# Where the gate products of a softmax attention stage are placed among its steps

## The chip, the cores and the metric

One core of a Trainium2 chip runs the whole program. The metric is the device time of one execution in microseconds (us), the median of several executions. Engines are named as the profile names them: PE (matmuls), PEld (PE's weight loads, which run beside the matmuls), DVE (VectorE), ACT (ScalarE), POOL (GpSimd), SP (which here issues most of the loads).

## The reference, cut to what matters

A trunk of two layers over 1040 frames of 1024 features. Each layer has an attention part and a gated feed-forward part. The attention part has two groups of heads that read the same normalised input: a gated linear attention ("GLA", 4 heads of 128 values) and a softmax attention with a forgetting bias ("FoX", 8 heads of 64). The GLA result is multiplied by a gate that comes from a product of its own:

```python
gq, gk, gv, gr, glr, fq, fk, fv, ff = jnp.split(xn @ w_in[i], cuts, axis=-1)
...
o_gla = rms_norm(o_gla, gla_norm[i].reshape(GLA_HEADS, GLA_DV)).reshape(B, L, GLA_WIDTH)
o_gla = o_gla * jax.nn.silu(gr)
...
h = h + jnp.concatenate([o_gla, o_fox], axis=-1) @ w_out[i]
```

The four 128-wide blocks of `gr` are the four gates of this document. Nothing of the softmax needs them: they are wanted only by the output projection `w_out`.

## The kernel before, in words

Activations lie transposed: features on 128 partitions, frames along the free dimension. Every dense product is made three times with split operands (high weight by high input, low by high, high by low: `mm3`, L254 to L256). One 128-wide weight tile by a chunk of frames takes 8 blocks of features, so 24 matmuls; the attention's products use the three chunks `CH_FOX` of 344, 348 and 348 frames.

Weights come by `weights` (called for each tile): two loads of 256 KB by SP (L212), for each half a cast to the high part on ACT (L221), and a subtraction for the low part (L223). The subtraction runs on POOL inside the attention stage (`self.att` set, `self.mixing` not) and on DVE elsewhere. There are three buffers each for high and low halves, so one tile and a half.

The attention stage of a layer runs GLA first. While the second pair of GLA heads is stepped through, the products of the first FoX head pair are made beside it, and at its end the weights of one more tile are already brought in (`coming`, next to the last `gla_steps`).

Then `fox` runs the softmax: four head pairs, each of 18 steps, from long rows of scores to short ones (row tiles 8 and 7, then 6 and 5, and so on, for two heads). One step is: scores on PE (L690, L691), bias and running minimum on DVE (L693), exponential on ACT (L705), two steps later transposes on PE (L726) that ACT and DVE copy and split (L368, L369), and three steps later the product with the values (L752). A loop over slots, `n` from 0, gives each slot one step and what earlier steps left due.

Beside the steps, dense products are dealt out as filler. A `Work` object is a queue of generators, one for each tile and chunk (`add_tile`, `unit`), with `left`, the summed cost in the kernel's own figures (`mm_us`, 3.54 us for a chunk of 348 frames). In every slot `fox` computes `fill_us`, the remaining cost over the remaining slots, and runs that much. `plan(p)` makes the queues: queue p begins at slot `starts[p]`, that is 4 slots after head pair p has begun (slots 4, 22, 40, 58), and the last at slot 62; what is left of the queue before is drained there. `plan(-1)` holds for slots 0 to 3 and is empty. Queues 0 to 2 hold the q, k and v products of the next head pair (9 chunks), then one gate (3 chunks). Queue 3 holds the last gate, and queue 4 the first part of the output projection. In `unit` the first use of a tile also starts the weights of the tile behind it in the same queue.

A gate chunk (`gr_products`) ends in an evacuation: DVE L650, L653, L657, L658, L659, L661, ACT L654 to L656, a load of the GLA result (L647, SP) and a store of the gated result (L663, POOL).

In this stage the order of instructions on an engine isn't the order of the source alone: the planner of the framework may issue an instruction ahead of its place when it takes its engine to be free, and prefers what stands earlier in the source. (The feed-forward stage writes PE's order by hand; the attention doesn't.) [...]

## Time and profile before

| what | us |
|---|---|
| median of 3 runs | 2505.76 (2503.37 to 2509.76) |
| the profiled execution, whole | 2508.55 |
| its span, first to last instruction | 2506.7 |
| PE busy in the span | 2470.6 |
| DVE busy | 1836.5 |
| ACT busy | 1296.8 |
| POOL busy | 385.6 |

The times of rows below count from the start of the span. The first layer's softmax begins its scores at 176.19 us. A busy PE is not PE at its peak: the profile models the ends of matmuls, and matmuls overlap one another. In the tables by stretch each engine has its busy time and, in brackets, its instructions that began in that stretch; then come the granted PE clock, the share of the DMA engines and what they moved.

### The profile page before, as it was taken

The page shows a single profiled execution, that of the slowest core. Times are in us where ns is not written, and L with a number is a line of the kernel's source. Part 1 is how long each engine was busy: PE and PEld are TensorE (multiplying, and loading weights), DVE is VectorE, ACT ScalarE, POOL GpSimd, SP SyncE. Part 2 cuts the span into 40 slices and gives each one's busy share as a digit, 9 for nine tenths or more (in the row PEclk, how much of TensorE's full clock was granted, in tenths as well). Part 3 has the DMA queues.
Part 4 walks back from the last instruction along what each step waited for, and adds up shares of the span by engine and source line. Part 5 has one row for each costly group of instructions (what it writes and reads, how often), then busy time and mean ns, then how long its engine had stood idle before and what let it go on. Part 6 is the DMA issues. An engine that isn't in the chain of part 4 may idle for free.

```text
span 2506.7 us, 47344 instructions
## 1 busy us (share of the span) xinstructions
PE 2470.6 (99%) x18358; PEld 2375.5 (95%) x18358; DVE 1836.5 (73%) x3739; ACT 1296.8 (52%) x2811; POOL 385.6 (15%) x567
## 2 busy tenths in 40 slices
PE   9999999999999999999999999999999999999998
PEld 8999999999999999999999899999999999997786
DVE  8656776869988888853566666777799888887535
ACT  7346666646555555641343566665465555555412
POOL 2023333210000000100211233431100000001002
PEclk9999999999999999999999999999999999999999
DMA  3132134343322224763312222143432222348622
GB/s 130 64 94 68 46 97 129 123 125 103 115 81 73 89 69 155 189 179 102 107 58 68 75 78 74 65 147 109 149 98 85 89 81 85 102 149 184 191 62 74
DMA packets 118546, 260.97 MB, mean 104 GB/s; under 512 B 14881, under 2 KB 32545, under 8 KB 118321
## 3 DMA queue, kind: packets, MB, share of 16 engines
q1 hardware_dynamic: 93984, 182.79, 23.5%
q0 software_dynamic: 22464, 72.84, 10.4%
q8 instruction: 144, 2.36, 0.4%
q10 hardware_dynamic: 1872, 2.31, 0.3%
q14 instruction: 82, 0.66, 0.1%
HBM read 177.29 MB, written 67.81 MB: 98 GB/s over the span
## 4 chain that ended last, share of the span: by engine, by line
PE 68%; issue 17%; DVE 9%; ACT 4%; DMA 2%; POOL 1%; SPq 0%; DVEq 0%; POOLq 0%; ACTq 0%
PE mm L254 7%; PE mm L256 7%; PE mm L255 7%; PE up L254 5%; PE up L255 5%; PE up L256 5%; PE down L254 5%; PE down L255 5%; PE down L256 5%; PE av L752 3%; PE tr L726 2%; DVE S L693 1%; PE wo L254 1%; PE wo L256 1%; PE wo L255 1%
## 5 line engine op out<-in xcount | busy, mean ns | idle before, releaser
L254 PE MATMUL up<-x,hi 128*128 128x260 f32 (+1 forms) x2240 | 634.0, 283 | 0.0
L256 PE MATMUL up<-x,hi 128*128 128x260 f32 (+1 forms) x2240 | 632.5, 282 | 0.7 <-DVE x L1157 0.7
L255 PE MATMUL up<-x,lo 128*128 128x260 f32 (+1 forms) x2240 | 632.5, 282 | 0.0
L256 PEld LDWEIGHTS up<-x,hi 128*128 128x128 f32 x2240 | 422.9, 189 | 1.1 <-DVE x L1157 0.9
L254 PEld LDWEIGHTS up<-x,hi 128*128 128x128 f32 x2240 | 422.2, 188 | 0.5 <-DVE hg L1370 0.2
L255 PEld LDWEIGHTS up<-x,lo 128*128 128x128 f32 x2240 | 422.5, 189 | 0.1
L254 PE MATMUL mm<-xh,hi 128*128 128x348 f32 (+4 forms) x1056 | 363.1, 344 | 0.0
L256 PE MATMUL mm<-xl,hi 128*128 128x348 f32 (+4 forms) x1056 | 340.0, 322 | 0.0
L255 PE MATMUL mm<-xh,lo 128*128 128x348 f32 (+4 forms) x1056 | 339.4, 321 | 0.0
L1133 DVE TENSOR_TENSOR lo<-raw,hi 128x512 fp32r<-128x512 f32 (+1 forms) x434 | 266.4, 628 | 81.0 <-ACT hi L1132 80.1
L1132 ACT CAST hi<-raw 128x512 fp32r<-128x512 f32 (+1 forms) x434 | 243.2, 572 | 148.1 <-PE up L256 88.7
L254 PEld LDWEIGHTS mm<-xh,hi 128*128 128x128 f32 x1056 | 199.6, 189 | 5.5 <-issue 4.6
L255 PEld LDWEIGHTS mm<-xh,lo 128*128 128x128 f32 x1056 | 199.5, 189 | 0.7 <-issue 0.7
L256 PEld LDWEIGHTS mm<-xl,hi 128*128 128x128 f32 x1056 | 198.4, 188 | 0.4 <-issue 0.3
L221 ACT CAST hi<-raw 128x512 fp32r<-128x512 f32 (+2 forms) x168 | 97.3, 580 | 187.4 <-PE down L256 106.0
L255 PE MATMUL down<-ah,lo 128*128 128x260 f32 (+1 forms) x528 | 168.8, 320 | 0.0
L254 PE MATMUL down<-ah,hi 128*128 128x260 f32 (+1 forms) x528 | 168.6, 319 | 0.0
L256 PE MATMUL down<-al,hi 128*128 128x260 f32 (+1 forms) x528 | 168.5, 319 | 0.0
L705 ACT ACTIVATE P<-S,m 116x460 f32<-116x460 f32 (+2 forms) x224 | 124.7, 561 | 71.7 <-DVE m L693 68.1
L369 DVE TENSOR_TENSOR PT<-tr,PT 116x464 fp32r<-116x464 f32 (+3 forms) x240 | 123.1, 516 | 47.3 <-ACT PT L368 45.7
L1114 DVE TENSOR_TENSOR raw<-raw,raw 128x512 f32<-128x512 f32 x198 | 135.3, 689 | 28.6 <-DMA raw<-in_wd_dram 26.4
L1395 POOL DMA_DIRECT2D actd<-cv x44 | 23.5, 535 | 744.4 <-DVE cv L1394 726.3
(308 smaller groups left out, 5974.7 us busy)
## 6 DMA issues: line engine op xcount, KB each, us to landing
raw<-in_wm_dram SPq DMA_DIRECT2D x330, 256.0 KB, 3.0
raw<-in_wd_dram SPq DMA_DIRECT2D x64, 256.0 KB, 3.5
actd<-cv POOLq DMA_DIRECT2D x22, 520.0 KB, 3.0
actd<-cv POOLq DMA_DIRECT2D x22, 512.0 KB, 3.0
cb<-cd SPq DMA_DIRECT2D x16, 520.0 KB, 3.8
st<-actd SPq DMA_DIRECT2D x14, 520.0 KB, 4.7
st<-actd SPq DMA_DIRECT2D x14, 512.0 KB, 5.0
kA<-kA SPq DMA_DIRECT2D x24, 260.0 KB, 4.1
```

Source lines behind the costliest of these rows:

```text
L221: nc.scalar.copy(hi[:, :n, :], raw[:, :n, :])
L254: nc.tensor.matmul(ps, wh, xh[:, c0:c0 + n], start=first, stop=False, skip_group_check=more)
L255: nc.tensor.matmul(ps, wl, xh[:, c0:c0 + n], start=False, stop=False, skip_group_check=more)
L256: nc.tensor.matmul(ps, wh, xl[:, c0:c0 + n], start=False, stop=last, skip_group_check=more)
L369: nc.vector.tensor_tensor(out=lo, in0=src, in1=hi.bitcast(F32), op=ALU.subtract)
L693: nc.vector.tensor_tensor_reduce(out=S[:rows, :n], in0=S[:rows, :n], in1=cb[:rows, c0:k1], scale=1.0, scalar=(BIG if ci == 0 else m[:rows, ...
L705: nc.scalar.activation(P[:rows, :n], S[:rows, :n], AF.Exp, scale=-1.0, bias=m[:rows, nch - 1:nch], accum_out=(den if nch == 1 else d3[:row ...
L726: nc.tensor.transpose(tr[:w, 3 - j, :rows], P[:rows, o:o + w], id_)
L752: nc.tensor.matmul(av[:, a:b], w.rearrange("p a b -> p (a b)"), x, start=(t == ts[0] and part == 0 and i == 0), stop=(t == last and i == 1))
L1114: nc.vector.tensor_tensor(out=q[out][:, :nk, :], in0=q[a][:, :nk, :], in1=q[b][:, :nk, :], op=op)
L1132: nc.scalar.copy(hi[:, :nk, :], src[:, :nk, :])
L1133: nc.vector.tensor_tensor(out=lo[:, :nk, :], in0=src[:, :nk, :], in1=hi[:, :nk, :].bitcast(F32), op=ALU.subtract)
```

## The change

The products of gate 0 move from the end of queue 0 to the queue of slots 0 to 3, which was empty; the weights that are brought in ahead during the GLA part are now those of gate 0 and no longer those of the q product of the second head pair. The six chunks of gates 1 and 2 are dealt out two to a queue: queue 0 ends with chunks 0 and 1 of gate 1, queue 1 with chunk 2 of gate 1 and chunk 0 of gate 2, queue 2 with chunks 1 and 2 of gate 2. A gate that is spread over two queues has its weights brought in twice. `tail` is the cost of the gate chunks at the end of a queue: while more than that is left, the rate is set so that the q, k and v products are done half a slot before the next head pair begins; the two gate chunks then go over the four slots that follow.

```diff
     def __init__(self):
-        self.q, self.left, self.boxes, self.debt = [], 0.0, [], 0.0
+        self.q, self.left, self.boxes, self.debt, self.tail = [], 0.0, [], 0.0, None
...
-    def gr_products(self, lyr, h, work, ap, pp, nm, dst=None):
+    def gr_products(self, lyr, h, work, ap, pp, nm, dst=None, w=None, chunks=CH_FOX):
...
-        self.add_tile(work, pp, self.wm[lyr, M_GR + h], nm["x"], CH_FOX if dst is None else CH_FOX[::-1], ev)
+        self.add_tile(work, pp, self.wm[lyr, M_GR + h], nm["x"], chunks, ev, w=w)
...
             fill_us = work.left / max(starts[p_next] - n, 1)
+            if work.tail is not None and work.left > work.tail:
+                fill_us = (work.left - work.tail) / max(first[p_next] - 0.5 - n, 0.5)
...
-                coming = {"src": self.wm[lyr, M_FQ + 1], "slots": None}
+                coming = {"src": self.wm[lyr, M_GR], "slots": None}
...
                     if p < 0:
-                        return w
-                    if p < 3:
-                        self.fox_products(lyr, p + 1, w, ap, pp, nm, qs[p + 1], None if p else coming["w"])
-                        self.gr_products(lyr, p, w, ap, pp, nm)
+                        self.gr_products(lyr, 0, w, ap, pp, nm, w=coming["w"])
+                    elif p < 3:
+                        self.fox_products(lyr, p + 1, w, ap, pp, nm, qs[p + 1])
+                        w.tail = -w.left
+                        for h, some in (((1, CH_FOX[:2]),), ((1, CH_FOX[2:]), (2, CH_FOX[:1])), ((2, CH_FOX[1:]),))[p]:
+                            self.gr_products(lyr, h, w, ap, pp, nm, chunks=some)
+                        w.tail += w.left
...
-                        self.gr_products(lyr, 3, w, ap, pp, nm, land[3])
+                        self.gr_products(lyr, 3, w, ap, pp, nm, land[3], chunks=CH_FOX[::-1])
```

## The prediction

> **What bounds the kernel now.** I read the page first, then the busy time by stretches through the softmax of each layer, then the waits of the worst stretch.
>
> ```profile
> PE 2470.6 (99%) x18358; PEld 2375.5 (95%) x18358; DVE 1836.5 (73%) x3739; ACT 1296.8 (52%) x2811; POOL 385.6 (15%) x567
> PE 68%; issue 17%; DVE 9%; ACT 4%; DMA 2%; POOL 1%; SPq 0%; DVEq 0%; POOLq 0%; ACTq 0%
> ```
>
> PE is busy for 99% of the span and carries 68% of the chain that ended last. The change takes no matmul away, so it can only win where PE loses time now. To find those places I compare stretches with a quiet one.
>
> ```profile
> 176.00:186.00 10.00, 9.76 (x62) 8.82 (x61) 5.73 (x22) 5.50 (x17) 3.73 (x5) 1.00 0.38 114
> 186.00:198.00 12.00, 10.77 (x74) 9.08 (x73) 8.78 (x30) 9.08 (x26) 4.50 (x7) 1.00 0.01 1
> 198.00:210.00 12.00, 11.66 (x89) 11.07 (x88) 8.76 (x27) 8.54 (x27) 2.60 (x4) 1.00 0.00 1
> ...
> 250.00:260.00 10.00, 10.00 (x66) 9.25 (x65) 7.99 (x28) 6.91 (x25) 2.72 (x5) 1.00 0.18 57
> 260.00:270.00 10.00, 9.88 (x68) 8.94 (x67) 9.66 (x30) 8.22 (x25) 3.41 (x6) 1.00 0.18 54
> 270.00:280.00 10.00, 10.00 (x75) 9.87 (x74) 8.50 (x28) 6.93 (x22) 3.21 (x5) 1.00 0.36 120
> ...
> 340.00:350.00 10.00, 9.89 (x67) 8.72 (x67) 9.72 (x31) 8.52 (x28) 2.83 (x4) 1.00 0.12 37
> 350.00:360.00 10.00, 10.00 (x76) 9.87 (x75) 9.66 (x32) 6.37 (x19) 3.82 (x6) 1.00 0.36 119
> ...
> 370.00:410.00 40.00, 39.89 (x288) 39.30 (x288) 22.55 (x75) 22.52 (x70) 16.32 (x23) 1.00 0.35 95
> ...
> 420.00:430.00 10.00, 9.86 (x66) 8.66 (x65) 9.71 (x35) 9.07 (x29) 2.33 (x5) 1.00 0.20 58
> ...
> 450.00:460.00 10.00, 8.25 (x61) 7.98 (x59) 10.00 (x33) 9.78 (x28) 3.16 (x6) 0.95 0.25 73
> ```
>
> After the bounds and the length stand PE, PEld, DVE, ACT and POOL. In the quiet stretch 370 to 410 weight loads run for 39.30 of 40 us, 98.3%, because nearly every matmul has one beside it; so a shortfall of PEld against 98.3% measures lost time even where PE still counts as busy. Three places stand out. **The early stretch**, the first eight steps of the first head pair: PE idles 0.24 + 1.23 + 0.34 = 1.81 us, and PEld falls short by 1.01 + 2.72 + 0.73 = 4.46 us. **The turns**, where a new head pair begins while the gate before it is still being made: there DVE is nearly full (9.66, 9.72 and 9.71 of 10). At the first turn PE idles 0.12 us and PEld is short by 0.58 + 0.89 = 1.47 us; the other two turns show 1.11 and 1.17 us in their worst ten us. **The end** (450 to 460), where PE idles 1.75 us; the work there is queue 4, which the change leaves alone.
>
> The second layer's early stretch, and what PE waits for in the first layer's:
>
> ```profile
> 1419.00:1429.00 10.00, 9.97 (x65) 9.02 (x63) 6.83 (x23) 6.08 (x18) 3.11 (x6) 1.00 0.24 79
> 1429.00:1441.00 12.00, 10.46 (x72) 8.94 (x71) 8.90 (x29) 9.14 (x29) 3.29 (x6) 1.00 0.00 1
> 1441.00:1453.00 12.00, 12.00 (x94) 11.78 (x93) 8.38 (x31) 8.69 (x28) 3.30 (x5) 1.00 0.07 23
> ```
>
> ```profile
> PEld S L690 <- ACT P L705: 2.3, 5, 0.9
> ...
> PE S L690 <- ACT P L705: 1.1, 2, 0.7
> ```
>
> Here the idle is 0.03 + 1.54 = 1.57 us and the shortfall 0.81 + 2.86 + 0.02 = 3.69 us. Between 186 and 198 PE waits for the exponentials of earlier scores: the softmax runs alone, with no dense matmul to put between. Why is there none?
>
> ```profile
> 176.19 0.45 PE L690 MATMUL S<-kA,qA 128*116 128x460 f32 x1
> ...
> 178.26 0.40 PE L254 MATMUL mm<-xh,hi 128*128 128x344 f32 x1
> ...
> 183.07 0.32 PE L255 MATMUL mm<-xh,lo 128*128 128x348 f32 x1
> 183.23 0.32 PE L256 MATMUL mm<-xl,hi 128*128 128x348 f32 x1
> ...
> 190.54 0.32 PE L254 MATMUL mm<-xh,hi 128*128 128x348 f32 x1
> ```
>
> This is PE in order of time. Step 0's scores start at 176.19. At 178.26, long before slot 4, q products of the second head pair begin: the planner already pulls filler into slots 0 to 3. That is two of nine chunks, gone by about 190, and then slots 4 to 6 find their share used up. The rows also give the price of filler: matmuls start 0.16 us apart, so a chunk is 24 x 0.16 = 3.8 us.
>
> **The change part by part.**
>
> *Gate 0 into slots 0 to 3.* It adds 3 x 3.8 = 11.5 us of PE work to the early stretch, against 1.8 idle or 4.5 short: ample. What its evacuation adds on the other engines:
>
> ```profile
> L650 DVE TENSOR_TENSOR gx<-mm,r x24: 506/510/518, 253.5 to 1695.1; 128x348 f32<-128x348 f32 x16, 128x344 f32<-128x344 f32 x8
> L653 DVE TENSOR_SCALAR ge<-gx x24: 328/338/1021, 254.5 to 1695.9; 128x348 f32<-128x348 f32 x16, 128x344 f32<-128x344 f32 x8
> L657 DVE TENSOR_TENSOR gog<-gx,gog x24: 505/510/516, 254.9 to 1696.2; 128x348 f32<-128x348 f32 x16, 128x344 f32<-128x344 f32 x8
> L658 DVE SCALAR_TENSOR_TENSOR ge<-ge,gy x24: 506/516/521, 257.1 to 1699.5; 128x348 f32<-128x348 f32 x16, 128x344 f32<-128x344 f32 x8
> L659 DVE SCALAR_TENSOR_TENSOR gy<-ge,gy x24: 510/521/1464, 257.7 to 1700.6; 128x348 f32<-128x348 f32 x16, 128x344 f32<-128x344 f32 x8
> L661 DVE SCALAR_TENSOR_TENSOR gog<-gy,gog x18: 500/514/603, 258.3 to 1678.0; 128x348 f32<-128x348 f32 x12, 128x344 f32<-128x344 f32 x6
> ```
>
> By the medians a gate chunk is 0.51 + 0.34 + 0.51 + 0.52 + 0.52 + 0.51 = 2.91 us of DVE, three are 8.7. The early 34 us hold 23.3 us of DVE now; 32.0 us in 34 + 11.5 - 3 = 42.5 us is 75%. ACT has 23.1 us there and room for three short operations a chunk. So the filler is covered, and what ends is the wait between 186 and 198. Bounds of the gain: the idle alone, 1.7 a layer (mean of 1.81 and 1.57), and the whole shortfall, 4.1 (4.46 and 3.69). I take the shortfall of the one stretch where the waits stand, 2.72 and 2.86: **2.8 us a layer**. The gate's load and store (SP, POOL) are the same instructions, earlier; nothing in slots 0 to 3 reads them.
>
> *One chunk fewer at each turn.* PE gives up 3.8 us, DVE 2.91. The first turn has DVE 7.99 + 9.66 + 8.50 = 26.15 of 30; afterwards it is 23.2 in 26.2, so 89% and not 87%: the turn gets shorter, not looser. Where DVE sets the pace, it shortens by 2.91 only and PE loses 3.8 - 2.9 = 0.9 more. Bounds a layer: a gain of all the shortfall (about 1.47 + 1.11 + 1.17 = 3.8) and a loss of 3 x 0.9 = 2.7. I take a gain of the idle only, 0.12 + 0.11 + 0.14 = **0.4 us a layer**: with DVE's share unchanged, the rest has no reason to go.
>
> *More weight loads.* Before, 11 tiles a layer pass through POOL; after, 13: gates 1 and 2 come twice. The q weights of the second pair no longer lie ready at slot 4.
>
> ```profile
> L221 ACT CAST hi<-raw x28: 607/620/661, 161.5 to 453.4; 128x512 fp32r<-128x512 f32 x28
> L223 POOL TENSOR_TENSOR lo<-raw,hi x22: 1272/1292/1419, 176.8 to 409.0; 128x512 fp32r<-128x512 f32 x22
> DMA to landing us min/median/max: 2.5/2.7/6.3
> ```
>
> A half costs 0.62 us on ACT and 1.29 on POOL, so the four new ones cost 2.5 and 5.2 us a layer. POOL is under 45% in every stretch quoted and hides its part; ACT has room in the quiet stretch (22.52 of 40), where two of the four casts fall, and less at a turn (9.07 of 10), where exponentials would queue behind the other two: 1.2 us at most, kept in the range. What they can cost PE besides comes by way of DVE:
>
> ```profile
> 267.08 1.46 DVE L659 SCALAR_TENSOR_TENSOR gy<-ge,gy 128x348 f32<-128x348 f32 x1
> ...
> 270.45 1.02 DVE L653 TENSOR_SCALAR ge<-gx 128x348 f32<-128x348 f32 x1
> ```
>
> ```profile
> 266.87 1.30 POOL L223 TENSOR_TENSOR lo<-raw,hi 128x512 fp32r<-128x512 f32 x1
> ...
> 269.96 1.30 POOL L223 TENSOR_TENSOR lo<-raw,hi 128x512 fp32r<-128x512 f32 x1
> ```
>
> Each of the two gate operations on DVE overlaps a subtraction on POOL and is longer than its median, by 0.94 and 0.68 us. [...] From the rows alone: bounds 0 and 4 x 0.94 = 3.8 us of DVE. Two of the four halves (gate 2's in queue 1) fall among gate operations, 2 x 0.81 = 1.6 us, and DVE is full in about a third of a turn: **0.5 us a layer lost**.
>
> *Sum.* 2.8 + 0.4 - 0.5 = 2.7 us a layer, 5.4 for both: the profiled execution goes from 2508.55 (span 2506.7 and 1.9 around it) to 2503.2. It ran 2.8 us above the median; from the median, 2505.76 - 5.4 = **2500.4 us**.
>
> **The rivals.**
>
> *Weights late (slower).* At slot 4 the q weights, and in slots 36 to 39 two tiles of a single chunk each, must be cast and subtracted while PE nears them; the second half waits for a buffer that the tile before still holds. With both halves exposed, 2 x (0.62 + 1.29) = 3.8 us at three places, 11.5 a layer less the 2.7: 17.6 us more, 2523. It wins from 0.9 us at each place on. Against it: at slot 22 the same happens today, and with the last gate chunk's matmul at 267.93 the next tile's begins here, scores and transposes filling the time between:
>
> ```profile
> 267.93 0.32 PE L256 MATMUL mm<-xl,hi 128*128 128x348 f32 x1
> ...
> 270.11 0.40 PE L254 MATMUL mm<-xh,hi 128*128 128x344 f32 x1
> ```
>
> *Turns starved (no change).* DVE sets the turns, the loss of 2.7 comes true: -2.8 + 2.7 + 0.5 = 0.4 a layer, 2506.6. For it: DVE at 97%. Against: PE still counts 9.86 or more of 10 there.
>
> *The planner undoes it (no change).* It already pulls filler forward, so gate 0 may only push out what was pulled, with the hole a few slots later: 2505.8. Against: slots 0 to 6 now own 11.5 us more.
>
> *All shortfall returns (faster).* 4.1 + 3.8 - 0.5 = 7.4 a layer: 2491.0. [...] The trace so far shows waits for only a part of it.
>
> **How the numbers follow.** Forecast (2 to 9 us gained) 0.46, weights late 0.17, the two of no change 0.24, all returned 0.13. About 0.3%, 7.5 us, is what a measurement of this kernel can tell from no change. Half of the forecast's chance lies beyond it: faster 0.23 + 0.13 = 0.36; same 0.23 + 0.22 = 0.45; slower 0.17 + 0.02 = 0.19. The range reaches from 2489 (all returned, with 2 us of spread between runs) to 2512 (no change, or one late tile a layer), and leaves out most of the slower rival, 0.18 in all. The interval of the forecast alone is 2497 to 2504.
>
> **What would show it.** Right: between the tenth and the twenty-second us of the first head pair PE has next to no wait for ACT, PEld is at 11.5 or more of 12, gate matmuls run from slot 0, and 26 subtractions on POOL a layer. Turns: the same DVE share in a shorter turn. Wrong: q matmuls of the second pair that wait for a subtraction (L223), a hole after slot 4 or at the turns, or L659 and L653 stretched more often. If PE's idle time in the early stretch goes and the time stays, the turns or the end took it.

## The result and the profile after

The changed kernel takes **2518.76 us** in the median of five runs (2516.5 to 2522.58); the kernel before takes 2509.76 in five runs (2503.37 to 2510.51). The ratio of the means is 1.0045, 95% interval 1.0034 to 1.0057: slower by under half a percent, where 2500.4 was predicted, a gain of 5.4 us. The profiled execution took 2518.76 us, its span 2517.0, which is 10.3 us more than before.

The page of the kernel after:

```profile
span 2517.0 us, 47386 instructions
...
PE 2470.7 (98%) x18358; PEld 2372.0 (94%) x18358; DVE 1842.4 (73%) x3739; ACT 1302.9 (52%) x2819; POOL 397.4 (16%) x575
```

PE runs the same 18358 matmuls and counts as busy for the same time, 2470.7 against 2470.6 us. So the 10.3 us are time in which PE idles that it did not idle before. I look for it where the change was made: first in the early stretch. The rows give, after the bounds and the length, PE, PEld, DVE, ACT, POOL, then granted clock, DMA share and GB/s (as in the prediction). The first head pair begins 1.75 us earlier than before, so the bounds are shifted by about 2.

```profile
174.00:184.00 10.00, 9.77 (x63) 8.88 (x62) 6.39 (x25) 5.01 (x16) 2.81 (x4) 1.00 0.34 114
184.00:196.00 12.00, 11.99 (x79) 10.84 (x78) 11.36 (x34) 9.94 (x28) 4.07 (x6) 1.00 0.18 53
196.00:208.00 12.00, 12.00 (x90) 11.70 (x88) 10.01 (x27) 8.06 (x21) 4.98 (x8) 1.00 0.24 82
```

PE is busy for 11.99 of the 12 us in which it idled 1.23 before; weight loads rose from 9.08 to 10.84, less than the 11.5 that the prediction set as a sign. This part of the change does what it says, though not in full. Then the places where a new head pair begins. From here on a **turn** is the stretch from the first scores of a head pair to those of its seventh step, six steps long; the other twelve steps are the **rest** of the pair. **Filler** is the dense matmuls of the queues alone. The bounds are read from PE's rows in time; for the first turn (second head pair) they are, before and after:

```profile
249.69 0.42 PE L690 MATMUL S<-kA,qA 128*116 128x460 f32 x1
...
279.32 0.38 PE L690 MATMUL S<-kA,qA 128*116 128x460 f32 x1
```

```profile
256.83 0.42 PE L690 MATMUL S<-kA,qA 128*116 128x460 f32 x1
...
284.61 0.38 PE L690 MATMUL S<-kA,qA 128*116 128x460 f32 x1
```

With such bounds, busy time by stretches for the first layer of the kernel before: opening of pair 0, its rest, turn 1, rest, turn 2, rest, turn 3.

```profile
176.19:200.02 23.83, 22.02 (x144) 19.01 (x142) 16.14 (x53) 15.95 (x47) 8.23 (x12) 1.00 0.16 49
200.02:249.69 49.67, 49.39 (x362) 48.62 (x361) 29.48 (x98) 30.41 (x91) 18.60 (x25) 1.00 0.29 80
249.69:279.32 29.63, 29.50 (x202) 27.68 (x202) 26.15 (x84) 21.53 (x70) 8.81 (x14) 1.00 0.24 78
279.32:331.38 52.06, 51.98 (x376) 51.19 (x375) 30.03 (x95) 30.99 (x91) 22.27 (x29) 1.00 0.27 79
331.38:360.96 29.58, 29.47 (x202) 27.65 (x202) 26.14 (x84) 21.53 (x70) 8.84 (x14) 1.00 0.23 78
...
413.03:443.35 30.32, 30.18 (x205) 28.20 (x205) 27.14 (x90) 23.88 (x75) 9.31 (x18) 1.00 0.40 134
```

And the same stretches of the kernel after:

```profile
174.44:204.81 30.37, 30.12 (x201) 27.87 (x199) 25.10 (x73) 21.36 (x60) 9.96 (x15) 1.00 0.27 89
204.81:256.83 52.02, 51.96 (x376) 51.16 (x375) 29.94 (x95) 30.63 (x90) 21.65 (x28) 1.00 0.28 82
256.83:284.61 27.78, 26.49 (x180) 23.80 (x178) 23.38 (x78) 20.78 (x68) 8.35 (x14) 1.00 0.22 66
284.61:336.68 52.07, 52.00 (x377) 51.21 (x375) 29.93 (x95) 30.75 (x90) 22.11 (x29) 1.00 0.28 81
336.68:365.57 28.89, 26.36 (x179) 23.85 (x179) 25.12 (x78) 21.59 (x70) 11.51 (x16) 1.00 0.26 83
...
417.65:447.95 30.30, 27.06 (x181) 24.27 (x181) 24.54 (x83) 22.23 (x72) 8.57 (x17) 1.00 0.43 142
```

These two tables are the whole result. Pair 0 grows from 73.50 to 82.39 us, by **8.89** for three chunks (24 matmuls at 0.16 us each, 3.84 us a chunk, 11.5 for three), so 2.6 us are won there. Each turn loses one chunk (turns 1 and 2 fall from 96 filler matmuls to 72, turn 3 from 99 to 75), and is shorter by **1.85, 0.69 and 0.02 us** where 3.84 were given up. The rests of the later pairs do not move. In the first layer this makes 8.89 - 2.56 = 6.3 us more; in the second the turns save 1.9, 0.7 and 1.61, which makes 4.7 more. From the first scores to the first output projection matmul of queue 4 the stage takes 285.9 and 284.2 us in the two layers against 279.3 and 279.5: 11.3 us of the span's 10.3. All else differs by one microsecond in sum, the other way (1947.0 us against 1948.0).

How to read the loss: PEld falls in turn 1 by 27.68 - 23.80 = 3.88 us, about the chunk that left, but the stretch shortens by 1.85 only. Against the quiet stretch's 98.3% the shortfall rises from 1.45 to 3.51 us. PE's idle time rises from 0.13 to 1.29 in turn 1, 0.11 to 2.53 in turn 2, 0.14 to 3.24 in turn 3. What left was work that had covered waits of the softmax; without it the waits show. In turn 1 ACT's exponentials wait for DVE's running minimum for 3.7 us in the kernel before and for 3.8 in the kernel after: that wait was there already, beside a busy PE.

DVE, which the prediction took to set the turns' pace, did lose its work as reckoned (26.15 to 23.38 in turn 1, where 23.2 was forecast), but its share of the turn fell to 84%, where 89% was forecast: the turn did not shorten as much as DVE's work.

What PE waits for in turn 1 of the kernel after (total, times, longest), which names only part of the 1.29 us:

```profile
PE tr L791 <- DVE PT L369: 0.5, 1, 0.5
PE S L690 <- ACT P L705: 0.5, 1, 0.5
```

No wait of a gate or q matmul for a cast or a subtraction stands there, in turns 2 and 3 or in the early stretch. Turn 3 of the first layer has a cause of its own: the bias rows of the last pair land late and PE stands for 2.21 us (last section); in the second layer, without that wait, turn 3 gave back 1.61.

### The profile page after: what moved, and what is told of

It reads as the page before. It is cut to its first block, busy times and chain, and to the rows that moved or that the text cites. A ratio compares the mean times of both kernels' runs of the same rounds, so it can differ in the third digit from the quotient of the medians.

```text
span 2517.0 us, 47386 instructions
## 1 busy us (share of the span) xinstructions
PE 2470.7 (98%) x18358; PEld 2372.0 (94%) x18358; DVE 1842.4 (73%) x3739; ACT 1302.9 (52%) x2819; POOL 397.4 (16%) x575
## 3 DMA queue, kind: packets, MB, share of 16 engines
q0 software_dynamic: 22464, 72.84, 10.3%
```

## The experiments

The theory after the result is **local worth**: a matmul given to a stretch where PE is full costs its 0.16 us, but a matmul taken out of a turn gives back less, because there the softmax's own way (scores, minimum, exponential, transposes, copies) and the gate's evacuation need the time anyway. What the edits do is read from the stage's length, because all else in the program takes 1942.5 to 1955.6 us in these kernels (those with other banks aside), a spread as large as the loss. Rivals, tried one after another: the second fetching of weight tiles; the way the filler is spread; the evacuation load on DVE and ACT; the number of score banks; too short a lag between the softmax's steps; the planner, which moves work between stretches.

This table has the lengths that the text below uses, in us, worked out as above from each run's rows. "Left" is the number of filler matmuls in turn 1. The stage is that of the first and second layer.

| run | pair 0 | turn 1 (left) | turn 2 | turn 3 | stage |
|---|---|---|---|---|---|
| before | 73.5 | 29.6 (96) | 29.6 | 30.3 | 279.3 / 279.5 |
| after | 82.4 | 27.8 (72) | 28.9 | 30.3 | 285.9 / 284.2 |
| e4_early_more | 82.4 | 29.6 (96) | 29.6 | 30.1 | 287.9 / 288.3 |
| e3_turn_less | 71.1 | 29.0 (87) | 29.0 | 31.1 | 271.6 / 272.3 |
| e1_even_pace | 79.7 | 29.0 (87) | 30.2 | 31.9 | 282.3 / 283.6 |
| e5_queue_from_0 | 75.6 | 29.2 (84) | 29.6 | 30.2 | 280.9 / 281.5 |
| e9_one_chunk_early | 73.8 | 29.6 (90) | 29.6 | 30.3 | 279.7 / 279.5 |
| e6_slim_after | 82.4 | 27.3 (72) | 26.3 | 30.0 | 282.4 / 280.2 |
| e7_slim_before | 73.5 | 29.5 (96) | 29.5 | 30.0 | 278.8 / 278.8 |
| e8_two_tiles_later | 82.4 | 27.8 (72) | 27.8 | 27.8 | 282.7 / 282.5 |

**The two halves of the change, one at a time.** The first kernel does the three chunks early and takes nothing away later: gate 0 is made twice, once in slots 0 to 3 and once where it was.

```diff
                     if p < 0:
+                        self.gr_products(lyr, 0, w, ap, pp, nm, w=coming["w"])
                         return w
                     if p < 3:
-                        self.fox_products(lyr, p + 1, w, ap, pp, nm, qs[p + 1], None if p else coming["w"])
+                        self.fox_products(lyr, p + 1, w, ap, pp, nm, qs[p + 1])
```

> The kernel before with gate 0 made once more in slots 0 to 3 (its products computed twice, queues 0 to 2 as before, the weights brought in ahead those of gate 0). The price of the early part alone: by the prediction 11.5 us of PE work less 2.8 to 3 us of filled waits, so 8 to 9 us a layer, less the 1.75 us by which the first scores begin earlier in the changed kernel: 14 to 17 us for both layers. If the q weights that are no longer ready at slot 4 cost something, more than 11.5 us a layer, 23 us and up. Head pair 0 becomes about 82 us, as in the changed kernel; pairs 1 and 2 stay at 81.7.

Measured 2522.34 us against 2507.7, ratio 1.0067 (1.0054 to 1.008): 14.6 us for six chunks of 3.84, and the stage is longer by 8.6 and 8.8 (all else was 3.9 us shorter in the profiled execution). The turns stay as they were. So the early term holds by itself: three chunks cost 8.7 us a layer in place of 11.5, and some 2.8 are won.

The second does the other half alone: before, with one chunk fewer in each of the first three gates, nothing moved and no tile brought in twice.

```diff
+                if c0 == CH_FOX[1][0]:
+                    nc.gpsimd.dma_start(self.mixd[h][:, c0 + n:T], og)
-        self.add_tile(work, pp, self.wm[lyr, M_GR + h], nm["x"], CH_FOX if dst is None else CH_FOX[::-1], ev)
+        self.add_tile(work, pp, self.wm[lyr, M_GR + h], nm["x"], CH_FOX[:2] if dst is None else CH_FOX[::-1], ev)
```

> The kernel before with the third chunk of gates 0 to 2 left out (its place in the stored mix is filled with the second chunk's values): every turn has one chunk less, nothing else is moved and no tile is brought in twice. If a chunk at a turn is worth its PE time, as the prediction had it, the time falls by 6 x 3.9 = 23 us, head pairs 1 and 2 from 81.7 to about 77.8 us. Theory 'starved turn': a chunk is worth 0.5 to 2 us there, pairs 1 and 2 stay above 79.5 us, and the time falls by 3 to 12 us only. Theory 'weights': since no tile is added here, the full 23 us.

Measured 2495.56 us, ratio 0.9955 (0.9943 to 0.9968): 12 us for six chunks worth 23 us of PE. The starved turn had 3 to 12 us, so this is its upper end, and pairs 1 and 2 fell to 78.3 us where it had them above 79.5. Nothing is fetched twice here, so the double fetching cannot be the main cause. Busy time of turn 1, the rest behind it, and turn 3:

```profile
246.80:275.76 28.96, 28.50 (x196) 26.48 (x196) 23.96 (x81) 21.49 (x70) 10.61 (x16) 1.00 0.26 77
275.76:325.14 49.38, 49.24 (x358) 48.48 (x357) 28.55 (x92) 30.02 (x88) 20.17 (x28) 1.00 0.30 84
...
403.51:434.56 31.05, 29.16 (x202) 27.53 (x202) 25.50 (x87) 22.84 (x74) 9.53 (x17) 1.00 0.42 142
```

The even pacing takes the 24 filler matmuls from both parts of the pair, 15 from the rest and 9 from the turn; three transposes that follow the v product move from the rest into the turn. So the rest does 18 matmuls fewer: its weight loads fall by 51.19 - 48.48 = 2.71 us and it shortens from 52.06 to 49.38, by 2.68: full worth. The turn does six fewer: its weight loads fall by 27.68 - 26.48 = 1.20 us and it shortens by 0.67, about half. That is local worth, seen on both sides in one run. The chunk's evacuation has left too, so this run doesn't tell the two reasons apart. Turn 3 even grows by 0.7; DVE waits 3.8 us for the bias rows there (see the last section).

**The same work, spread evenly.** After, without the tail's own pace:

```diff
-                        w.tail = -w.left
...
-                        w.tail += w.left
```

> The changed kernel without the pacing of the queues: the eleven chunks of queues 0 to 2 go evenly over 18 slots (2.16 us of filler a slot, and no longer 2.36 until half a slot before the next pair and 1.77 after). Theory 'starved turn' (a turn has too little dense work beside a softmax that is paced by DVE and ACT, so a chunk taken from it saves much less than its 3.8 us of PE): head pairs 1 and 2 stay within 1.5 us of the changed kernel's 79.8 and 81.0 us and the time stays some 8 to 12 us above the kernel before. Theory 'pacing' (the slower rate in the four slots of the turn makes the hole): pairs 1 and 2 fall to about 77.9 us each (before less one chunk), and the time is 2 to 6 us under the kernel before. Theory 'weights' (tiles brought in twice, POOL stretching DVE): no change against the changed kernel, pair 2 stays about 1 us above pair 1.

Measured 2512.93 us, ratio 1.0024 (1.0015 to 1.0033), half of the loss; of the three expectations none had it (8 to 12 us slower, 2 to 6 faster, or no change against the kernel after).

```profile
253.97:282.95 28.98, 28.51 (x196) 26.51 (x196) 23.97 (x81) 21.49 (x70) 10.08 (x15) 1.00 0.23 67
282.95:332.34 49.39, 49.24 (x359) 48.48 (x357) 28.55 (x92) 30.02 (x88) 20.09 (x28) 1.00 0.31 83
```

The turn keeps 87 filler matmuls and the quiet rest gives up 15: together 3.3 us saved, where the change as made saves 1.85. The spread matters, as local worth has it. Turns 2 and 3 eat part of it (30.2 and 31.9; in turn 3 DVE waits 4.6 us for the bias rows), so the stage remains 3.0 and 4.1 us longer than before.

**Fill the early stretch from queue 0 instead, or with one chunk.** Two milder ways to use the early idle time: before, with queue 0 beginning at slot 0, and after, with one gate chunk early and two left in queue 0.

```diff
-        starts = [f + 4 for f in first] + [first[3] + 8, len(steps) + 8]
+        starts = [0] + [f + 4 for f in first[1:]] + [first[3] + 8, len(steps) + 8]
```

> The kernel before with queue 0 begun at slot 0 and not at slot 4: the same twelve chunks, in the same order, over 22 slots (1.93 us a slot for 2.36). It fills the early stretch from the quiet one and leaves three chunks' worth of work to turns 2 and 3. Theory 'starved turn' with the early gain real: faster than the kernel before by 2 to 5 us if turn 1 keeps enough work, no change if what is gained early is lost at turn 1 (whose rate falls too). If the planner pulls filler forward anyway and the queue's start doesn't matter: no change, head pair 0 stays 73.5 us.

```diff
-                        self.gr_products(lyr, 0, w, ap, pp, nm, w=coming["w"])
+                        self.gr_products(lyr, 0, w, ap, pp, nm, w=coming["w"], chunks=CH_FOX[:1])
...
+                        self.gr_products(lyr, p, w, ap, pp, nm, chunks=CH_FOX if p else CH_FOX[1:])
```

> A version that could beat both: of gate 0 only the first chunk goes to slots 0 to 3, its other two stay at turn 1, gates 1 and 2 lie whole at turns 2 and 3 as in the kernel before, and the queues go evenly over their 18 slots. If the first chunk in the early stretch fills the waits that the three chunks of the changed kernel filled (2.8 us of 11.5), it costs 1 to 2 us there, and the chunk taken out of queue 0 evenly saves 3.3 us (what it saved where a chunk was left out of the kernel before): 1 to 2 us a layer, 2 to 4 in all, faster than the kernel before. If the chunk costs its 3.8 us early, or the gate's weights, now brought in twice, stretch DVE: no change or up to 3 us slower.

Measured 2512.46 (1.0021, 1.0013 to 1.003) and 2508.39 (1.0005, 0.9996 to 1.0014). The first is slower, which neither expectation had. 28 more filler matmuls come into the opening of pair 0 and cost 4.7 us there (23.83 to 28.53), more than their 4.5 us of PE; but PE waits 1.2 us there for a load of `kL`, the low part of the keys, a wait that the kernel before doesn't have, so this run does not tell what such filler is worth there. In the second, pair 0 takes 73.8 and the turns are what they were: nothing won, nothing lost.

**Is it the gate's evacuation?** Both kernels without the gates' sigmoid for the gates at the turns; what is left out stands in the expectations.

```diff
+            if h in (1, 2):
+                nc.vector.tensor_tensor(out=og, in0=x, in1=og, op=ALU.mult)
+                nc.gpsimd.dma_start(self.mixd[h][:, c0:c0 + n], og)
+                return
             nc.vector.tensor_scalar(out=e, in0=x, scalar1=-87.0, scalar2=None, op0=ALU.max)
```

> The changed kernel with the evacuation of gates 1 and 2, those that lie at the turns, cut to two operations on DVE (L650 and L657) and none on ACT: the sigmoid of these two gates is left out. PE's work, its stores and its weight loads stay. To be read beside the same cut in the kernel before. A turn is counted from the first scores of a head pair to those of its seventh step: 29.6 us for turns 1 and 2 before, 27.75 and 28.9 after, so the chunk that left saved 1.85 and 0.7 of its 3.8 us. Theory 'DVE and ACT pace the turn': without that load turns 1 and 2 fall to about 24.5 us, and the difference to the kernel before with the same cut is about 3.8 us, a chunk's whole PE time. Theory 'order' (the waits come from the order that the planner wrote, not from the load on DVE and ACT): turns stay within 0.7 us of 27.75 and 28.9.

> The kernel before with the same cut of the evacuation, for gates 0 to 2 (the three that lie at its turns; their sigmoid is left out). Theory 'DVE and ACT pace the turn': the three turns fall from 29.6 us by the 1 to 1.5 us that PE loses there, to some 28.2; the time by 6 to 9 us. Theory 'order': turns within 0.5 us of 29.6. In both, a difference to the changed kernel with the same cut of 3.8 us a turn says that the chunk's worth comes back once DVE and ACT are light, one of 1.9 that it doesn't.

Measured 2509.79 (1.0012, 1.0002 to 1.0021) for after, and 2506.68 (1.0001, 0.9992 to 1.0011) for before. Turn 1 and turn 2 of the slim kernel after, then turn 1 of the slim kernel before:

```profile
256.88:284.13 27.25, 26.04 (x179) 23.83 (x178) 20.38 (x70) 19.36 (x63) 8.73 (x15) 1.00 0.22 71
...
336.20:362.54 26.34, 25.70 (x179) 23.84 (x179) 20.40 (x70) 19.82 (x65) 11.03 (x17) 1.00 0.28 93
```

```profile
247.79:277.26 29.47, 29.28 (x202) 27.56 (x202) 21.53 (x72) 19.26 (x63) 9.25 (x16) 1.00 0.26 83
```

With 96 filler matmuls the turn does not care: 4.6 us of DVE's work go and it shortens by 0.16. "DVE is full at 97% of ten us" was no sign of a DVE-paced turn. With 72 it does care: 0.53 us in turn 1, 2.55 in turn 2. So part of what a chunk fails to give back is the evacuation, more at turn 2. Over all six turns of both layers the chunks give back 6.7 of 23.0 us with the evacuation and 13.1 with the slim one: 6.4 of the 16.3 us that fail to come back go with it. But in turn 1 the chunk is still worth only 29.47 - 27.25 = 2.22 of 3.84 us with DVE at 75% (at turn 2 it is 29.54 - 26.34 = 3.20). **1.6 us in turn 1 are not the evacuation.**

Where they are lost shows when turn 1 is cut in two, at the scores of its fourth step. The slim kernel before, then the slim kernel after:

```profile
247.79:261.21 13.42, 13.29 (x89) 12.21 (x88) 9.93 (x37) 8.46 (x31) 2.80 (x6) 1.00 0.24 79
261.21:277.26 16.05, 16.00 (x116) 15.35 (x115) 11.60 (x36) 10.81 (x33) 6.45 (x10) 1.00 0.27 86
```

```profile
256.88:270.75 13.87, 12.68 (x84) 11.16 (x84) 10.66 (x38) 9.60 (x35) 4.07 (x7) 1.00 0.22 69
270.75:284.13 13.38, 13.36 (x96) 12.67 (x95) 9.73 (x32) 9.76 (x29) 4.66 (x8) 1.00 0.21 73
```

Half of the chunk leaves each part. In the last three steps weight loads fall by 2.68 us and the time by 2.67: full worth. In the first three they fall by 1.05 and the time *grows* by 0.45: no worth at all. (Turn 2, cut the same way: 2.37 and 2.50 in the last three, 1.37 and 0.70 in the first.) The first step alone says why: from its scores to the next it takes 3.81 us in the kernel before and in the slim one, with 15 filler matmuls, and 3.79 in the kernel after and its slim form, with 12, and in e3 with 11. The first step's three chunks hold all three score banks, and one comes free for the second step's scores with the first step's exponential (kernel after):

```profile
260.63 0.47 PE L690 MATMUL S<-kA,qA 128*116 128x460 f32 x1 [0.48 <-ACT P L705]
```

So the softmax's own way sets the length of that step, and fewer than 15 filler matmuls in it only leave PE idle. With the evacuation on, both parts lose: the first three steps take 13.65 us before and 15.08 after, the last three 15.98 and 12.70, where weight loads change by +0.32 and -4.21.

**The tile fetched twice at turn 2.** In the change, queue 1 ends with two single chunks of two gates; here they come to queue 2.

```diff
-                        for h, some in (((1, CH_FOX[:2]),), ((1, CH_FOX[2:]), (2, CH_FOX[:1])), ((2, CH_FOX[1:]),))[p]:
+                        for h, some in (((1, CH_FOX[:2]),), ((2, CH_FOX[:2]),), ((1, CH_FOX[2:]), (2, CH_FOX[2:])))[p]:
```

> The changed kernel with the two chunks of a queue dealt out otherwise: queue 0 chunks 0 and 1 of gate 1, queue 1 chunks 0 and 1 of gate 2, queue 2 chunk 2 of gates 1 and 2. All sums are as in the changed kernel; the turn with two tiles, and so with two more subtractions on POOL, is now turn 3 and not turn 2. Theory 'a second tile costs a turn about 1.2 us': turn 2 falls from 28.9 to about 27.75 us, head pair 2 from 81.0 to about 79.8, turn 3 becomes about 1.2 us longer, and the time stays. Theory 'turns get longer one by one, whatever their tiles': turn 2 stays at 28.9.

Turn 2 now is turn 1's twin, with two fewer subtractions on POOL (8.31 us of POOL and not 11.51); turn 3, which has the two tiles here, is the second row:

```profile
338.13:365.89 27.76, 26.70 (x179) 23.80 (x179) 23.38 (x78) 20.86 (x68) 8.31 (x14) 1.00 0.22 72
...
417.97:445.72 27.75, 26.84 (x182) 24.25 (x181) 23.97 (x83) 22.14 (x72) 12.36 (x18) 1.00 0.45 153
```

So the second tile cost turn 2 28.89 - 27.76 = 1.13 us. At turn 3 the two tiles cost nothing that shows, though 1.2 us were expected: it takes 27.75 us, as turn 2. (The 30.30 of the kernel after are no measure for it, they hold PE's wait of 2.21 us behind the bias rows; at that place PE waits 0.91 in e8.) The difference between the two turns goes with whether gate operations are stretched beside a subtraction. In the kernel after's turn 2, DVE's and POOL's rows:

```profile
343.59 1.60 DVE L657 TENSOR_TENSOR gog<-gx,gog 128x348 f32<-128x348 f32 x1
...
348.57 1.47 DVE L661 SCALAR_TENSOR_TENSOR gog<-gy,gog 128x348 f32<-128x348 f32 x1
```

```profile
343.40 1.41 POOL L223 TENSOR_TENSOR lo<-raw,hi 128x512 fp32r<-128x512 f32 x1
...
348.23 1.44 POOL L223 TENSOR_TENSOR lo<-raw,hi 128x512 fp32r<-128x512 f32 x1 [0.20 <-ACT hi L221]
```

Two gate operations of 0.51 us take 1.60 and 1.47, each over a subtraction that began 0.2 and 0.3 us earlier; in turns 2 and 3 of e8_two_tiles_later no gate operation takes over 0.52 us. The prediction's two rows (1.46 and 1.02 us) lie the same way, begun 0.2 and 0.5 us after a subtraction. The 2.05 us more of DVE became 1.13 of the turn (the second tile's casts on ACT are in the 1.13 too). Where the turn has 96 filler matmuls, as before, two such stretched operations (1.46 and 1.02 us) stood in turns 1 and 2 and cost next to nothing, as e7 shows.

The stage is shorter than in the kernel after by 3.2 and 1.7 us, but the median, 2519.49 (1.0046, 1.0032 to 1.0059), is not. All else took 8.6 us more in the profiled execution (1955.6 against 1947.0). Part of that is in the feed-forward, which neither edit touches: its second set of down products waits 5.8 us here, 2.3 in the kernel after and 0.0 before.

```profile
L254 PE MATMUL down<-ah,hi 128*128 128x260 f32 (+1 forms) x528 | 169.6, 321 | 5.8 <-DVE h L1673 3.5 <-ACT do L1675 2.3
```

Why is not settled, nor where the other 5 us are. For that reason the stage lengths and not the medians carry the comparisons between edits of 1 or 2 us.

**More lag, more banks, no planner.** Can the 1.6 us be had back? Three pairs of kernels, each an edit made to before and to after, so that what a chunk is worth at a turn can be read from the difference. Lag: transposes, value products and stores one step later, six buffers for the exponentials, and the sigmoid cut in all gates (further buffers that grow with it are left out here).

```diff
-            at(n + 2, f"T{ci}", T_(ci, P))
+            at(n + 3, f"T{ci}", T_(ci, P))
...
-            at(n + 3, f"av{ci}", av(ci))
+            at(n + 4, f"av{ci}", av(ci))
...
-P_BUFS = 5
+P_BUFS = 6
```

> The changed kernel with all four gates' evacuation cut to two operations (the sigmoids are left out, which frees the room for a sixth buffer of exponentials) and one more slot between the scores of a step and its transposes, and so before its product with the values. Beside e6, whose turns 1 and 2 took 27.25 and 26.3 us for the same dense work. Theory 'chain' (what PE waits for at a turn is the softmax's own way from scores over DVE and ACT back to PE, with too little dense work in between): the longer distance takes the waits away, turn 1 falls by 1 us or more, to 26.2 or less, with 72 dense matmuls as before. Theory 'order' (the planner's list has the waits, however long the distance): turns 1 and 2 stay within 0.4 us of 27.25 and 26.3.

> The kernel before with the same two edits (sigmoids left out, one more slot of distance). Beside e7, whose turn 0 took 23.85 us and whose turns 1 and 2 took 29.5. Theory 'chain': turn 0, which has the waits between 186 and 198 us, falls by 1 us or more, turns 1 and 2 by less than 0.7, since 96 dense matmuls cover the way already. Theory 'order': turn 0 stays within 0.4 us of 23.85.

One run each: 2521.61 and 2511.06 beside 2512.04. Turns 1 and 2 take 29.2 and 29.5 in after and 29.7 and 29.8 in before, so a chunk is worth only 0.6 and 0.3 us; but a new wait of PE stands in both (transposes of the store behind an exponential, 4.1 us in three waits of the first layer in after, 3.6 in before). In after the granted clock is 0.94 in both turns besides. The opening of pair 0 in before fell from e7's 23.85 to 22.61 us, as the theory 'chain' had it; turn 1 of after, which should have fallen to 26.2 or less, grew to 29.2, as no theory had it. **Inconclusive** for the turns: the lag brought a wait of its own.

Banks: one PSUM bank for the dense products and four for the scores.

```diff
-        tags = ("mm", "mm", "S", "S", "S")
+        tags = ("mm", "S", "S", "S", "S")
...
-            pp = PsumTags({"mm": (pp2, 2), "S": (pp1, 3), "tr": (pp2, 2), "av": (pp1, 1)})
+            pp = PsumTags({"mm": (pp2, 1), "S": (pp1, 4), "tr": (pp2, 2), "av": (pp1, 1)})
```

> The kernel before with the eight PSUM banks of the attention dealt out otherwise: four for scores (three before), one for dense products (two before). PE's waits of the early stretch and of the turns name ACT's exponential or DVE's splits as what releases a scores or transpose bank. Theory 'banks' (PE is held because no scores bank is free, and a fourth one lets it go on): turn 0 falls from 23.83 us by 1 us or more, and if the single dense bank costs little, the time falls by 2 to 5 us. Theory 'rate' (DVE and ACT empty the banks at the rate that they have, and one bank more only moves the wait): turn 0 within 0.5 us of 23.83; each chunk's end, 0.5 us until DVE has read it, now may hold the next chunk, up to 40 x 0.5 = 20 us slower for a layer if nothing stands between.

> The changed kernel with the same four and one banks. Theory 'banks': turns 1 and 2 fall from 27.75 and 28.9 us by 1 us or more each, and the difference to the kernel before with the same banks is nearer to a chunk's 3.8 us. Theory 'rate': the turns stay within 0.5 us, or get longer, and the difference to the kernel before with the same banks stays under 2.5 us.

Measured 2577.98 (1.0274, 1.0256 to 1.0291) and 2587.22 (1.0315, 1.03 to 1.0331). Turns 1 and 2 take 31.55 and 31.56 in before, 29.97 and 29.24 in after: a chunk is worth 1.6 us (turn 1 of after ran at a clock of 0.94) and 2.3 us, and 2.7 at turn 1 of the second layer. With a fourth score bank the full 3.8 do not come back, so too few banks alone is not the cause. For the first step it is the cause: with 7 to 10 filler matmuls it takes 2.32 to 2.80 us in after and no longer 3.8, but PE then idles in the second and third step (1.8 to 2.1 us together). The edit costs more than anything else tried (the rest takes 54.4 and not 52.06; one dense bank is the likely reason, not tried by itself), which blurs the comparison.

Planner: PE keeps the order of the source in the softmax.

```diff
-                self.fox(lyr, ap, pp, qs, plan, lambda: box["mix"][KD - 1])
+                with tc.manual_schedule(engines={mybir.EngineType.PE}):
+                    self.fox(lyr, ap, pp, qs, plan, lambda: box["mix"][KD - 1])
```

> The kernel before with PE's instructions of the softmax stage kept in the order of the source (the other engines are planned as ever): no filler is pulled forward, slots 0 to 3 have none. Theory 'planner' (holes come from filler pulled forward): the eight steps after slot 4 have their filler, the turns fall below 29.6 us, and the time falls. Theory 'softmax pace': turn 0, with no filler in its first four slots, still takes 20 us or more, turns 1 and 2 stay at 29 to 30.5 us. If the planner's order was worth something, the stage gets longer by 2 to 10 us a layer.

> The changed kernel with PE's order of the source in the softmax stage. Theory 'planner': with filler where the source has it, a chunk less at turns 1 and 2 saves about 3.8 us against e14. Theory 'softmax pace': it saves 1 to 2.5 us against e14, as with the planner.

Measured 2534.7 (1.0101, 1.0086 to 1.0116) and 2555.99 (1.0186, 1.0166 to 1.0205). Turn 1 in source order, before and then after:

```profile
255.12:286.18 31.06, 29.89 (x207) 28.10 (x207) 26.58 (x84) 21.87 (x69) 8.93 (x15) 1.00 0.28 84
```

```profile
262.52:296.20 33.68, 28.03 (x185) 25.43 (x183) 24.73 (x78) 20.04 (x66) 8.19 (x13) 0.95 0.19 59
```

Here a turn with a chunk *less* takes 2.6 us *longer*. (In before the turns at 31.0 and the stage, 11.3 and 12.4 us longer, lie above what either theory gave.) So the planner does not cause the loss; in its order, where later matmuls are pulled into the holes, the same turns are shorter. PE's rows at the longest hole, then DVE's and POOL's inside it, show what a turn with thin filler is made of:

```profile
273.21 0.32 PE L256 MATMUL mm<-xl,hi 128*128 128x348 f32 x1
278.00 0.31 PE L719 MATMUL tr<-ident,Ps 116*116 116x116 f32 x1 [4.47 <-ACT P L705]
```

```profile
274.38 1.55 DVE L661 SCALAR_TENSOR_TENSOR gog<-gy,gog 128x344 f32<-128x344 f32 x1
...
276.79 0.33 DVE L693 CUSTOM_DVE_ANT_0 S<-S,cb,m 116x116 f32<-116x116 f32 x1
```

```profile
274.31 1.26 POOL L223 TENSOR_TENSOR lo<-raw,hi 128x512 fp32r<-128x512 f32 x1 [4.92 <-ACT hi L221]
```

The last filler matmul of its slot is out, the next in order are the transposes of a step whose exponential isn't ready, and PE stands for 4.47 us. The exponential in turn waits for the step's third minimum on DVE (276.79), and in front of that DVE works off the gate's evacuation, with one operation stretched to 1.55 us beside a subtraction: about 1.8 of the 4.47 us are gate operations (0.25 of L659, 1.55 of L661). So the hole is the softmax's way with the gate's evacuation in it, and not the softmax's way alone; that the 1.6 us in the planned order, which stay with a slim evacuation, are its thinned remainder is an inference.

## Why the prediction was wrong

**The early term was right.** 2.8 us a layer were forecast, 2.6 measured in the change (11.5 - 8.89) and 2.8 with that part alone; PE's wait for the exponentials between the tenth and the twenty-second us is gone and POOL runs 26 subtractions a layer, as forecast. One sign failed: PEld is at 10.84 of 12 there and not at 11.5 or more, so that stretch gained 1.76 us of weight loads where 2.72 were counted on; the twelve us behind it, which were not counted, added 0.63. That the term came so near is in part luck.

**The step that failed is "One chunk fewer at each turn".** It said that PE gives up 3.8 us and that, with DVE's share unchanged, "the rest has no reason to go", and took a gain of 0.4 us a layer on top. It booked the full 3.84 us of each chunk as returned. Measured, a chunk gave back 1.85, 0.69 and 0.02 us in the first layer and 1.9, 0.7 and 1.61 in the second: instead of 0.4 won, 9.0 and 7.3 us were lost. About 2.0 us fail to come back at each turn; turn 2 loses 1.1 more to its second tile, and turn 3 of the first layer 1.6 more where the bias rows are late, a term that the prediction did not have. Two errors stand behind the 2.0. The turns showed PE idle for 0.12 us because they *had* 96 filler matmuls; the idle time of a stretch is no bound on what it will idle with fewer. And DVE's 9.7 of 10 was taken as the turn's pace, so that the worst case was 0.9 us a turn; e7 shows that DVE did not pace the turn before, and e6 that its load explains only a part of the loss after. Even with a slim evacuation, filler that left the first three steps of a turn gave back nothing (turn 1) or half its time (turn 2), because there the softmax's own way sets the pace, which is shown for the first of these steps.

**The rival "turns starved" named the right place with the wrong price.** It gave 2.7 us a layer and ended at no change; 9.0 and 7.3 put it on the slower side. What spoke for it was in the profile, in PEld's shortfall of 1.47 us, and what was held against it (PE busy 9.86 of 10) was no evidence. Its reason, DVE as the pace, holds for at most the 6.4 of 16.3 us that went with the evacuation's load on DVE and ACT.

**The two remaining terms.** The double weight loads were put at 0.5 us a layer; e8 gives 1.13 for turn 2. It came the way that was forecast (gate operations stretched beside a subtraction, by 1.09 and 0.96 us), though before has two such at turns 1 and 2 as well, and the share of it that reaches the turn was 55% and not a third. Of the prediction's two rows, L659 reads two tiles and L653 one, and both were stretched (by 0.94 and 0.68 us). "Weights late" and "the planner undoes it" did not happen: no dense matmul waits for a cast or a subtraction in the first layer's turns, and pair 0 kept its 2.6 us. The shortfall of weight loads, which the rival "all shortfall returns" counted as its gain, did not come back but grew, from 1.45 to 3.51 us in turn 1: here it was no stock to draw on, it measured how thin the cover was.

**The sum with the measured terms.** First layer 2.6 - 9.0 = -6.4 (measured -6.6 in the stage), second 2.6 - 7.3 = -4.7 (measured -4.7). The turns' term is measured here as a whole, so the sum closes by its making and proves no cause.

**What stays open.** Of the 2.0 us that turn 1 fails to give back, e6 and e7 put 0.4 on the evacuation; the 1.6 left are lost in the turn's first three steps. The first of these is shown to be the softmax's own pace (0.48 us of idle time, the same with a slim evacuation). For the other two, too few score banks alone and the planner are set aside, the lag run brought a wait of its own, and PE's named waits (0.3 and 0.5 us for copies on DVE) cover only a part. No version beat the kernel before: e9_one_chunk_early and e7_slim_before (which leaves work out) tie with it.

## What to carry to other kernels

Price filler where it leaves as well as where it goes: here 24 matmuls cost 8.9 / 3 = 3.0 us where PE had idled, were worth their full time in the quiet rest (18 matmuls, 2.68 us), and gave back 0.0 to 1.9 us at a turn. A stretch that shows no idle time *with* its cover may be one long wait without it, so before work is taken from it, measure the same stretch with a little less (e3 did that in one run: 1.20 us of weight loads out, 0.67 us back), and read it step by step: a step whose length stays the same with more and with less filler has its pace from elsewhere. A busy share near 100% on another engine isn't proof that it sets the pace: take its work away and see whether the stretch moves.

## What the runs showed of the hardware

After some holes in the matmuls the granted PE clock was lower. In e15's turn 1, busy time in pieces of two us:

```profile
274.50:276.50 2.00, 0.00 (x0) 0.00 (x0) 2.00 (x4) 0.07 (x1) 1.99 (x3) 1.00 0.00 0
276.50:278.50 2.00, 0.50 (x4) 0.50 (x5) 1.65 (x8) 1.28 (x5) 0.30 (x1) 1.00 0.62 219
278.50:280.50 2.00, 2.00 (x9) 1.78 (x9) 0.43 (x3) 1.11 (x5) 0.00 (x0) 0.51 0.33 79
280.50:282.50 2.00, 1.79 (x7) 1.36 (x6) 1.87 (x5) 0.17 (x1) 0.00 (x0) 0.64 0.03 10
```

After the 4.47 us without a matmul the clock is 0.51 and 0.64 for four us, and the dense matmuls that take 0.32 to 0.41 us before the hole (272.80 to 273.21) take 0.48 to 0.49 there (281.03 to 281.61): about 1.7 us of matmul time lost (an estimate, 2.00 x 0.49 + 2.00 x 0.36); so even without it e15's turn 1 (33.68) would be longer than e14's (31.06). The length of the hole alone does not decide it: 2.21 us in the kernel after's turn 3 and 2.53 in e6's (both first layer) left the clock at 1.00, and soon after a hole of 1.64 us in e10's turn 1 it was 0.50:

```profile
262.74 0.42 PE L782 MATMUL tr<-ident,fon 116*128 116x116 f32 x2 [1.64 <-ACT P L696]
```

```profile
265.00:267.00 2.00, 2.00 (x9) 1.77 (x9) 1.40 (x4) 1.22 (x5) 0.42 (x1) 0.50 0.15 59
```

One load landed late, perhaps because of its neighbours. The bias rows (cb, 520 KB) of the last pair landed 5.4 to 5.6 us after their issue before, and in the kernel after:

```profile
DMA to landing us min/median/max: 7.9/8.1/8.2
```

```profile
420.18 0.65 DVE L693 CUSTOM_DVE_ANT_0 S<-S,cb 116x460 f32<-116x460 f32 x1 [2.54 <-DMA cb<-cd]
...
423.19 0.47 PE L690 MATMUL S<-kA,qA 128*116 128x460 f32 x1 [2.21 <-ACT P L705]
```

DVE waits 2.54 us for them and PE 2.21 behind it: that is in turn 3 of the first layer, the one that gave nothing back. Before, the third of the 520 KB loads of `h` that POOL issues there came after both bias loads (410.40, against issues at 407.25 to 409.6); after, at 413.31, between the two (411.85 and 414.2). In the second layer they landed after 5.9 to 6.5 us and turn 3 took 28.51. That the order of these issues is the reason was not tried, and it is not the whole: e8 has the load of `h` between the two as well (413.63, between 412.2 and 414.5), and there they landed after 6.9 to 7.1 us and DVE did not wait for them.
